# Output projection as seven half-size products of 512 columns, with two weight sums and the adds of x in accumulating DMAs

## The chip, the cores and the metric

The kernel runs on one core of one Trainium2 chip. The metric is the device time of one execution in microseconds (us). Before the change the median of three runs is 432.96 us (432.49 to 433.72). The profile is one more execution, taken by the hardware profiler: its time is 432.8 us, and the span that the profile covers is 431.1 us, so 1.7 us lie around the span.

## What is computed

One decoder block on x of 512 rows and 1024 columns, all float32. The reference, cut to what the change touches:

```python
proj = rms_norm(x, norm_g) @ w_in            # queries, keys, values, gates
y_fox, y_moba = ...                          # two attention branches, 512 x 512 each
merged = (sigmoid(ga + b_gate[0]) * (y_fox @ w_fox)
          + sigmoid(gb + b_gate[1]) * (y_moba @ w_moba))   # 512 x 1024
x = x + merged @ w_out                       # w_out: 1024 x 1024
```

The change is about the last line: the product of `merged` (512 x 1024) with `w_out` (1024 x 1024), and the add of x.

## The kernel before

Every matrix product is done in three matmuls. Each float32 operand is split in a high part and a low part (ScalarE copies to the matmul type `F32R`, VectorE subtracts), and high x high, high x low and low x high are added up in PSUM. A weight piece is 128 partitions x 4 rows of k x 256 columns (512 KB). Its raw form is tagged `wr` (4 buffers), its two parts `wh` and `wl` (4 buffers each). `split` at line 131 makes the parts: line 134 on ScalarE, line 136 on VectorE. `stream` and `pump` keep the list of loads (SP queue) and splits in order and ahead of use.

The kernel has stages: projections, attention with projections in between, "gates" (the groups GA0, GA1, GB0, GB1) and "end". The groups of the gates (`group`, line 703) already compute a product of half-size blocks by seven products in place of eight (Strassen-Winograd): the sums S1 to S4 of the activations lie ready in tiles `S0h` to `S3l`, and the sums of the weights are made in place by VectorE at line 711. Each of their matmuls has 256 columns.

The wm units (`unit_m`, line 807) multiply the second branch by `w_moba` into a PSUM bank `pm` (12 matmuls of 512 columns a unit), VectorE multiplies by the gate and adds the first branch (lines 813 and 814), and ScalarE and VectorE split the result in the parts `mgh` and `mgl` (lines 819 and 820). The eight column blocks of `merged` are so kept in `MG[0]` to `MG[7]`, transposed, 128 x 512 each; blocks 0, 1, 4, 5 come from wm0 and wm2 in stage "gates", and blocks 2, 3, 6, 7 from wm1 and wm3 in stage "end".

The output product follows. `w_out` is taken in four column blocks of 256 (wo0 to wo3), each in two pieces. `first_o` (line 824) does wo0 into four banks at once, block by block as `merged` becomes ready; `unit_o` (line 838) does the rest, one bank of 128 rows x 256 columns after the other. That is 4 column blocks x 4 row blocks x 8 blocks of k x 3 = 384 matmuls of 256 columns, named `po`. `out_o` (line 853) loads a piece of x on the SP queue, adds it to the bank on VectorE (line 857) and stores it from ScalarE's queue (line 858), 128 KB each.

A scheduler orders the instructions of an engine when the program is built; on the chip each engine takes its queue in that order, and an instruction that waits holds all behind it.

Of the kernel before, what the change touches and what calls it, by code (L numbers as in the profile page):

```python
# [19 lines left out]
CW = 256  # L20
# [3 lines left out]
WR = 4  # L24
# [5 lines left out]
def fox_moba_kernel(ctx: ExitStack, tc, xT, x, w_in, w_fl, w_fox, w_moba, w_out, cst, rope, out):  # L30


    nc = tc.nc
    V, A, G, T = nc.vector, nc.scalar, nc.gpsimd, nc.tensor

    con = ctx.enter_context(tc.tile_pool(name="con", bufs=1))
    sb = ctx.enter_context(tc.tile_pool(name="sb", bufs=1))
# [3 lines left out]
    stage = {}  # L41
# [46 lines left out]
    cs = con.tile([P, C_END], F32, name="cs")  # L88
# [17 lines left out]
    for i in range(WARM):  # L106
# [10 lines left out]
    Gh = con.tile([P, KT, S], F32R, name="Gh")  # L117
    Gl = con.tile([P, KT, S], F32R, name="Gl")
# [10 lines left out]
    chunks = {}  # L129

    def split(src, n, name, half=False):
        hi = sb.tile([P, 4, 264], F32R, name=f"wh_{name}", tag="wh", bufs=4)
        lo = sb.tile([P, 4, 264], F32R, name=f"wl_{name}", tag="wl", bufs=4)
        A.activation(hi[:, :, 0:n], src, AF.Copy)  # L134
        for eng, q in ((V, slice(0, 2)), (G, slice(2, 4))) if half else ((V, slice(0, 4)),):
            eng.tensor_tensor(out=lo[:, q, 0:n], in0=src[:, q], in1=hi[:, q, 0:n].bitcast(F32), op=OP.subtract)  # L136
        return hi, lo
# [24 lines left out]
    COLS = {}  # L162
# [13 lines left out]
    loads, preps, first_prep = [], [], {}  # L176
    done = {"loads": 0, "preps": 0}

    def pump(i):

        while True:
            j = done["loads"]
            if j < len(loads) and (j < WR or loads[j - WR][1] < done["preps"]):
                loads[j][0]()
                done["loads"] += 1
            elif done["preps"] < len(preps) and done["preps"] <= i + 3:
                preps[done["preps"]]()
                done["preps"] += 1
            else:
                return  # L190

    def stream(name):
        first_prep[name] = len(preps)
        if name[0] == "G":
            group(name)
            return
        w, n, cnt = ((w_fox, int(name[2]), 1) if name[:2] == "wf" else (w_moba, int(name[2]), 1) if name[:2] == "wm"
                     else (w_out, int(name[2]), 2) if name[:2] == "wo" else (w_in, COLS[name] // CW, 2))
        for hf in range(cnt):
            raw = {}  # L200

            def load(hf=hf, raw=raw):
                raw[0] = sb.tile([P, 4, CW], F32, name=f"wr_{name}{hf}", tag="wr", bufs=WR)
                nc.sync.dma_start(out=raw[0], in_=w[n, :, 4 * hf:4 * hf + 4, :])

            def prep(hf=hf, raw=raw):
                chunks.setdefault(name, []).append(split(raw[0], CW, f"{name}{hf}", HALF[0] and name[1] in "qkvz"))
            loads.append((load, len(preps)))
            preps.append(prep)
# [4 lines left out]
    r = con.tile([P, NT], F32, name="r")  # L214
# [33 lines left out]
    HT = S // 2  # L248
# [420 lines left out]
    FS, MG = {}, {}  # L669

    def br_mm(p, name, br, c):
        hi, lo = chunks[name][0]
        cc = slice(c * P, (c + 1) * P)
        for k in range(4):
            yh, yl = Y[br, k]
            T.matmul(p, hi[:, k, cc], yh, start=(k == 0), stop=False)  # L676
            T.matmul(p, hi[:, k, cc], yl, start=False, stop=False)  # L677
            T.matmul(p, lo[:, k, cc], yh, start=False, stop=(k == 3))  # L678
# [14 lines left out]
    SG = {}  # L693
# [7 lines left out]
    groups = {}  # L701
# [104 lines left out]

    def unit_m(i, c):
        def go():
            j = 2 * i + c
            p = pj(f"pm{j}")  # L810
            br_mm(p, f"wm{i}", "m", c)
            u = SG[i][:, c, :]
            V.tensor_tensor(out=u, in0=p, in1=u, op=OP.mult)
            V.tensor_tensor(out=u, in0=u, in1=FS[i][:, c, :], op=OP.add)
            if i % 2:
                mh_, ml_ = (stage["pool"].tile([P, S], F32R, name=f"mg{hl}{j}", tag="mg", bufs=8) for hl in "hl")
            else:
                mh_, ml_ = (t2("y", 15, f"mg{hl}{j}", dt=F32R) for hl in "hl")
            A.activation(mh_, u, AF.Copy)
            V.tensor_tensor(out=ml_, in0=u, in1=mh_.bitcast(F32), op=OP.subtract)  # L820
            MG[j] = (mh_, ml_)
        return go

    def first_o():
        banks = [pst(tg, 2, f"po0_{i}") for i, tg in enumerate(("pj", "pj", "lg", "lg"))]
        for kk in range(KT):
            hi, lo = chunks["wo0"][kk // 4]
            gh, gl = MG[kk]
            k = kk % 4
            for t in range(NT):  # L830
                st = slice(t * P, (t + 1) * P)
                T.matmul(banks[t][:, :CW], gh[:, st], hi[:, k, :CW], start=(kk == 0), stop=False)
                T.matmul(banks[t][:, :CW], gh[:, st], lo[:, k, :CW], start=False, stop=False)
                T.matmul(banks[t][:, :CW], gl[:, st], hi[:, k, :CW], start=False, stop=(kk == KT - 1))
        for t in range(NT):
            out_o(banks[t], 0, t)

    def unit_o(n, t):
        def go():
            p = pj(f"po{n}{t}")  # L840
            st = slice(t * P, (t + 1) * P)
            for hf in range(2):
                hi, lo = chunks[f"wo{n}"][hf]
                for k in range(4):
                    kk = 4 * hf + k
                    gh, gl = MG[kk]
                    T.matmul(p[:, :CW], gh[:, st], hi[:, k, :CW], start=(kk == 0), stop=False)  # L847
                    T.matmul(p[:, :CW], gh[:, st], lo[:, k, :CW], start=False, stop=False)  # L848
                    T.matmul(p[:, :CW], gl[:, st], hi[:, k, :CW], start=False, stop=(kk == KT - 1))  # L849
            out_o(p, n, t)  # L850
        return go

    def out_o(p, n, t):
        xr = t2("pt", 4, "xr")[:, :CW]
        nc.sync.dma_start(out=xr, in_=x[t * P:(t + 1) * P, n * CW:(n + 1) * CW])
        o = t2("u", 4, "ot")
        V.tensor_tensor(out=o[:, :CW], in0=p[:, :CW], in1=xr, op=OP.add)  # L857
        nc.scalar.dma_start(out=out[t * P:(t + 1) * P, n * CW:(n + 1) * CW], in_=o[:, :CW])


    order = ["fqa", "fka", "fza", "fzb", "fva", "fqb", "fkb", "fvb", "mqa", "mka", "mva", "mza", "mqb", "mkb", "mvb", "mzb", "wf0", "wf1", "wf2", "wf3",
             "GA0", "GA1", "GB0", "wm0", "wm2",
             "GB1", "wm1", "wm3", "wo0", "wo1", "wo2", "wo3"]
    for nm in order[2:]:
        stream(nm)

    def units(name):
        k = name[:2]
        if k[0] == "G":
            return groups[name]  # L870
        if k == "wf":
            return [unit_f(int(name[2]), c) for c in range(2)]
        if k == "wm":
            return [unit_m(int(name[2]), c) for c in range(2)]
        if k == "wo":
            return [unit_o(int(name[2]), t) for t in range(4)]
# [28 lines left out]
    def seq(names):  # L905
        for u in filler(names):
            u()
# [32 lines left out]
    for n in range(4):  # L940
# [9 lines left out]
        if n == 0:  # L950
            for k in range(4):
                store = []

                at = 3 * k + 5
# [21 lines left out]
            gate[0]()  # L976
    seq(["wm0", "wm2", "GB1"])
    enter("end")
    seq(["wm1", "wm3"])
    pump(first_prep["wo0"])  # L980
    first_o()
    seq(["wo1", "wo2", "wo3"])
    stage.pop("guard").__exit__(None, None, None)


# [58 lines left out]
```

## Time and profile before

| | before |
|---|---|
| median of three runs | 432.96 us |
| time of the profiled execution | 432.8 us |
| its span | 431.1 us |
| TensorE busy | 424.4 us |
| VectorE busy | 308.5 us |
| ScalarE busy | 253.9 us |
| GpSimd busy | 87.8 us |
| first matmul of the output product starts | 373.41 us |
| last matmul of the output product starts | 427.15 us |

The lines of the profile stand with the prediction below. PE is TensorE, PEld its weight loads, DVE is VectorE, ACT is ScalarE, POOL is GpSimd, SP is the engine whose queue issues most loads; POOLq, ACTq and SPq are the queues. A row of the timeline gives the start in us, the duration in us, the engine, the line, the operation, and the output tile with its inputs. A row of the groups ends with the count, then the busy time in us and the mean duration of one in ns, then the idle time before them and what ended it.

### The profile page before, as it was taken

How to read it: one execution, taken by the hardware profiler on the slowest of the kernel's cores; microseconds unless marked ns; L12 is line 12 of the kernel's file. 1: busy time of each engine (PE TensorE's matmuls, PEld its weight loads, DVE VectorE, ACT ScalarE, POOL GpSimd, SP SyncE). 2: the span in 40 equal slices, each digit the busy share in tenths (PEclk: the TensorE clock that was granted, in tenths of full speed). 3: DMA queues.
4: the chain of work that ended last, by engine and by line, in shares of the span. 5: the costliest groups of instructions: out<-in, count | busy, mean ns of one | idle time of the engine just before them, and what ended most of it. 6: DMA issues, size and time to landing. Idle time of an engine off the chain costs nothing.

```text
span 431.1 us, 8090 instructions
## 1 busy us (share of the span) xinstructions
PE 424.4 (98%) x3103; PEld 400.7 (93%) x3103; DVE 308.5 (72%) x551; ACT 253.9 (59%) x488; POOL 87.8 (20%) x108
## 2 busy tenths in 40 slices
PE   8999999999999999999999999999999999999996
PEld 6998899999999998999998888899999989999996
DVE  5669976869979867767856896859897796673311
ACT  4986336876867867667765876647645545531100
POOL 1049200227044650045630103020000000000000
PEclk9999999999999999999999999999999999999999
DMA  7981235236565414304304305271415206525231
GB/s 239 398 296 57 80 116 152 74 103 205 166 209 185 130 45 123 122 3 126 117 15 136 109 13 200 99 263 51 141 55 196 98 2 210 189 95 166 85 94 45
DMA packets 25670, 56.13 MB, mean 130 GB/s; under 512 B 3240, under 2 KB 11872, under 8 KB 25632
## 3 DMA queue, kind: packets, MB, share of 16 engines
q1 hardware_dynamic: 14528, 40.08, 27.8%
q10 hardware_dynamic: 9952, 11.34, 8.8%
q0 software_dynamic: 1152, 4.19, 2.7%
q8 instruction: 24, 0.39, 0.4%
q14 instruction: 14, 0.11, 0.1%
HBM read 46.01 MB, written 6.32 MB: 121 GB/s over the span
## 4 chain that ended last, share of the span: by engine, by line
PE 84%; DVE 7%; DMA 5%; ACT 2%; issue 1%; SPq 1%; DVEq 0%; ACTq 0%
PE pb_GB L750 3%; PE pb_GA L750 3%; PE pb_GA L747 3%; PE pb_GB L749 3%; PE pb_GB L747 3%; PE pb_GA L749 3%; PE po L847 3%; PE po L849 3%; PE po L848 3%; PE pv L608 2%; PE pv L607 2%; PE lg L553 2%; PE lg L552 2%; PE pm L676 2%; PE pm L677 2%; PE pm L678 2%
## 5 line engine op out<-in xcount | busy, mean ns | idle before, releaser
L331 POOL TENSOR_TENSOR ff<-ss,mh 128x8 f32<-128x8 f32 x16 | 28.6, 1793 | 65.6 <-DVE ss L329 65.1
L557 ACT ACTIVATE p<-p,negm 128x128 f32<-128x128 f32 (+1 forms) x64 | 35.7, 559 | 9.7 <-DVE negm L555 8.2
L555 DVE CUSTOM_DVE_ANT_0 p<-lg,mask 128x128 f32<-128x128 f32 (+1 forms) x64 | 30.9, 485 | 14.4 <-PE lg L553 13.7
L847 PE MATMUL po<-wh_wo,mgh 128*128 128x256 f32 x96 | 27.1, 282 | 0.0
L849 PE MATMUL po<-wh_wo,mgl 128*128 128x256 f32 x96 | 27.0, 282 | 0.0
L848 PE MATMUL po<-wl_wo,mgh 128*128 128x256 f32 x96 | 27.0, 281 | 0.0
L857 DVE TENSOR_TENSOR ot<-po,xr 128x256 f32<-128x256 f32 x16 | 6.6, 424 | 24.7 <-PE po L849 23.5
L136 DVE TENSOR_TENSOR wl_GA<-wr_ga,wh_GA 128x1024 fp32r<-128x1024 f32 x14 | 17.9, 1294 | 5.7 <-ACT wh_GA L134 3.6
L134 ACT ACTIVATE wh_wo<-wr_wo 128x1024 fp32r<-128x1024 f32 x8 | 8.5, 1061 | 21.6 <-PE po L849 8.0
L552 PE MATMUL lg<-KH,QS 128*128 128x128 f32 (+1 forms) x64 | 20.5, 329 | 0.0
L134 ACT ACTIVATE wh_GA<-wr_ga 128x1024 fp32r<-128x1024 f32 x14 | 14.6, 1059 | 9.2 <-PE pb_GA L749 4.6
L136 DVE TENSOR_TENSOR wl_GB<-wr_gb,wh_GB 128x1024 fp32r<-128x1024 f32 x14 | 16.8, 1222 | 4.2 <-ACT wh_GB L134 3.3
L134 ACT ACTIVATE wh_GB<-wr_gb 128x1024 fp32r<-128x1024 f32 x14 | 14.6, 1060 | 8.6 <-PE pm L677 2.5
L633 DVE TENSOR_TENSOR ypair<-pv,ysh 64x512 f32<-64x512 f32 x16 | 11.0, 688 | 11.2 <-ACT ysh L632 11.0
L847 PEld LDWEIGHTS po<-wh_wo,mgh 128*128 128x128 f32 x96 | 18.1, 189 | 0.0
L848 PEld LDWEIGHTS po<-wl_wo,mgh 128*128 128x128 f32 x96 | 18.1, 189 | 0.0
L849 PEld LDWEIGHTS po<-wh_wo,mgl 128*128 128x128 f32 x96 | 18.1, 188 | 0.0
L136 DVE TENSOR_TENSOR wl_wo<-wr_wo,wh_wo 128x1024 fp32r<-128x1024 f32 x8 | 9.8, 1222 | 7.4 <-ACT wh_wo L134 7.4
L604 DVE TENSOR_TENSOR ptl<-p_a,pth 128x512 fp32r<-128x512 f32 x16 | 11.0, 686 | 4.7 <-ACT pth L603 4.7
L526 DVE SCALAR_TENSOR_TENSOR QS<-p_qT,cs,QS 64x512 fp32r<-64x512 f32 x16 | 12.0, 750 | 2.5 <-ACT QS L525 2.1
L750 PE MATMUL pb_GA<-Gh,wl_GA 128*128 128x256 f32 x48 | 13.6, 283 | 0.0
L749 PE MATMUL pb_GA<-Gl,wh_GA 128*128 128x256 f32 x48 | 13.5, 281 | 0.0
(447 smaller groups left out, 1764.5 us busy)
## 6 DMA issues: line engine op xcount, KB each, us to landing
wr_ga<-in_w_in_dram SPq DMA_DIRECT2D x8, 512.0 KB, 3.5
wr_gb<-in_w_in_dram SPq DMA_DIRECT2D x8, 512.0 KB, 4.1
wr_wo<-in_w_out_dram SPq DMA_DIRECT2D x8, 512.0 KB, 3.8
xt<-in_xT_dram SPq DMA_DIRECT2D x8, 256.0 KB
x<-in_x_dram SPq DMA_DIRECT2D x8, 256.0 KB, 7.5
KH<-KH ACTq DMA_DIRECT2D x16, 128.0 KB, 2.4
s_dramh<-sum_sh ACTq DMA_DIRECT2D x8, 256.0 KB
s_draml<-sum_sl ACTq DMA_DIRECT2D x8, 256.0 KB, 3.5
```

The costliest lines, as they stand in the source:

```text
L134: A.activation(hi[:, :, 0:n], src, AF.Copy)
L136: eng.tensor_tensor(out=lo[:, q, 0:n], in0=src[:, q], in1=hi[:, q, 0:n].bitcast(F32), op=OP.subtract)
L331: G.tensor_tensor(out=f2, in0=ss.rearrange("p t h -> p (t h)"), in1=mh, op=OP.pow)
L552: T.matmul(lg[:, :n], qs[:, qt], kh[:, :n], start=True, stop=False)
L555: V.tensor_tensor_reduce(pt, lg[:, :n], mask[:, 512 - n:512], -0.125, 3.0e38, op0=OP.add, op1=OP.min, accum_out=mkn[:, hh, i:i + 1])
L557: A.activation(pt, pt, AF.Exp, bias=mkn[:, hh, i:i + 1], scale=-1.0, accum_out=rs[:, hh, i:i + 1])
L747: T.matmul(o, hi[:, k, cc], lh, start=(n < 3 and c == 0 and k == 0), stop=False, skip_group_check=True)
L749: T.matmul(o, hi[:, k, cc], ll, start=False, stop=False, skip_group_check=True)
L750: T.matmul(o, lo[:, k, cc], lh, start=False, stop=(k == 3), skip_group_check=True)
L847: T.matmul(p[:, :CW], gh[:, st], hi[:, k, :CW], start=(kk == 0), stop=False)
L848: T.matmul(p[:, :CW], gh[:, st], lo[:, k, :CW], start=False, stop=False)
L849: T.matmul(p[:, :CW], gl[:, st], hi[:, k, :CW], start=False, stop=(kk == KT - 1))
```

## The change

The output product is computed in half-size blocks: `merged` in four blocks A11 to A22 of 256 rows x 512 of k, and `w_out` in four blocks of 512 x 512. Seven products take the place of eight. Four of them have sums of the blocks of `merged` on the left (S1 to S4), four have sums of the blocks of `w_out` on the right (T1 to T4). The left block is the stationary operand, and one matmul takes 512 columns of the right block, which lie as two runs of 256 in the weight tile. There are 7 x 2 x 4 x 3 = 168 of them.

- VectorE makes S1 to S4 from the merged blocks (`sum_o`: 8 subtractions or adds of 128 x 512), ScalarE and VectorE split them (`parts_o`: 8 each) into the tiles `Gh` and `Gl`, which held the normalised input until then.
- `T1` = B12 - B11 and `T3` = B22 - B12: ScalarE negates the raw piece in place, and a DMA issued from GpSimd adds the other block from `w_out` to it in memory (`minus`; 4 DMAs of 512 KB). `T2` = B22 - T1 and `T4` = B21 - T2 are made by VectorE (`sub`; 4 of 128 x 1024).
- The raw pieces are 8 loads of 512 KB as before, four of them into four new buffers of the stage "end" (tag `wx`). There are 14 splits of weight pieces in place of 8.
- ScalarE copies a block's PSUM banks to a tile `eo` (`keep`; 8 of 128 x 512), a DMA from GpSimd adds the piece of x to it (8 of 256 KB), and VectorE adds the last PSUM bank to that (`result`), from where it is stored. The 16 loads of x on the SP queue are gone. The last store is cut in two halves, of which the second goes out from SP.
- Of the merged blocks 0 to 3 only 256 rows are still split; blocks 4 to 7 as before.
- Part of the work is kept behind VectorE's last instruction of the moment (`behind()`), which ties the order in its queue.

```diff
@@ def unit_m: cut in merge_a (matmuls, lines 813 and 814) and merge_b (split)
+            n = HT if j < 4 else S
...
+            A.activation(mh_, u[:, 0:n], AF.Copy)
+            V.tensor_tensor(out=ml_, in0=u[:, 0:n], in1=mh_.bitcast(F32), op=OP.subtract)
...
-    def first_o():
...
-    def unit_o(n, t):
...
-    def out_o(p, n, t):
...
+    def sum_o(m, what):
+        a, b = SG[m], SG[m + 2]
+        x, y, op = {"S1": (a[:, :, HT:S], b[:, :, HT:S], OP.add), "S2": (SF.get((m, "S1")), a[:, :, 0:HT], OP.subtract),
+                    "S4": (b[:, :, 0:HT], SF.get((m, "S2")), OP.subtract),
+                    "S3": (a[:, :, 0:HT], a[:, :, HT:S], OP.subtract)}[what]
...
+        V.tensor_tensor(out=f, in0=x, in1=y, op=op)
+    def parts_o(m, what):
+        f = SF[m, what]
+        hi, lo = (so(what, q)[:, 2 * m:2 * m + 2, :] for q in range(2))
+        A.activation(hi, f, AF.Copy)
+        V.tensor_tensor(out=lo, in0=f, in1=hi.bitcast(F32), op=OP.subtract)
+    O_PRODUCTS = (("A11", "11", 1), ("A12", "21", 2), ("S4", "22", 4), ("S3", "T3", 3), ("S2", "T2", 1),
+                  ("S1", "T1", 1), ("A22", "T4", 3))
...
+        def minus(key, c, plus):
+            A.activation(R[key, c], R[key, c], AF.Copy, scale=-1.0)
+            G.dma_start(out=dst(key, c), in_=src(plus, c), accum_op=OP.add)
+        def sub(key, c, x, y):
+            V.tensor_tensor(out=wide(R[key, c]), in0=wide(R[x, c]), in1=wide(R[y, c]), op=OP.subtract)
+        def prep(n, c):
...
+                A.activation(wide(hi), wide(R[key, c]), AF.Copy)
+                V.tensor_tensor(out=wide(lo), in0=wide(R[key, c]), in1=wide(hi).bitcast(F32), op=OP.subtract)
...
+        def product(n):
...
+            for t in range(2):
+                o = b[at][t].rearrange("p (n c) -> p n c", n=2)
+                for k in range(4):
...
+                    T.matmul(o, gh, hi[:, :, r, :], start=(new and k == 0), stop=False, skip_group_check=True)
+                    T.matmul(o, gh, lo[:, :, r, :], start=False, stop=False, skip_group_check=True)
+                    T.matmul(o, gl, hi[:, :, r, :], start=False, stop=(k == 3), skip_group_check=True)
+        def keep(at, tq, cq):
...
+                A.activation(e[at][:, t, :], b[at][t], AF.Copy)
+                t0 = tq * HT + t * P
+                G.dma_start(out=e[at][:, t, :], in_=x[t0:t0 + P, cq * 512:(cq + 1) * 512], accum_op=OP.add)
+        def result(bb, ee, tq, cq, parts=1):
...
+                    V.tensor_tensor(out=o[:, c:c + n], in0=b[bb][t][:, c:c + n], in1=e[ee][:, t, c:c + n], op=OP.add)
+                    eng = nc.scalar if c == 0 else nc.sync
+                    eng.dma_start(out=out[t0:t0 + P, cq * 512 + c:cq * 512 + c + n], in_=o[:, c:c + n])
...
-    seq(["wm1", "wm3"])
-    pump(first_prep["wo0"])
-    first_o()
-    seq(["wo1", "wo2", "wo3"])
+    groups["WO"]()
+    def behind():
+        return tc.issue_after(last_on(mybir.EngineType.DVE))
...
+        evac(2)
+        with behind():
+            sub("22", "22", "11")
+            parts_o(1, "S2")
+        evac(1)
+        prep(4)
+        product(3)
+        evac(3)
+        with behind():
+            parts_o(1, "S1")
+            prep(5)
+        product(4)
+        evac(4)
+        with behind():
+            sub("21", "21", "22")
+        prep(6)
+        product(5)
+        result(1, 4, 0, 1)
+        result(1, 3, 1, 1)
+        product(6)
+        evac(6)
```

More of the change, by code (lines that the diff above doesn't have):

```diff
@@ L196, in stream @@
             return
+        if name == "WO":
+            group_o()
+            return
         w, n, cnt = ((w_fox, int(name[2]), 1) if name[:2] == "wf" else (w_moba, int(name[2]), 1) if name[:2] == "wm"
-                     else (w_out, int(name[2]), 2) if name[:2] == "wo" else (w_in, COLS[name] // CW, 2))
+                     else (w_in, COLS[name] // CW, 2))
         for hf in range(cnt):
@@ L808, in go, with merge_a @@
         def go():
+            merge_a(i, c)
+            merge_b(i, c)
+        return go
+    def merge_a(i, c):
+        if True:
             j = 2 * i + c
@@ L814, in go @@
             V.tensor_tensor(out=u, in0=u, in1=FS[i][:, c, :], op=OP.add)
-            if i % 2:
-                mh_, ml_ = (stage["pool"].tile([P, S], F32R, name=f"mg{hl}{j}", tag="mg", bufs=8) for hl in "hl")
-            else:
[L818 to L822, printed above, removed]
-    def first_o():
[L825 to L836, printed above, removed]
@@ L838, in unit_o @@
-    def unit_o(n, t):
[L839 to L851, printed above, removed]
@@ L853, in out_o, with merge_b @@
-    def out_o(p, n, t):
[L854 to L858, printed above, removed]
+    def merge_b(i, c):
+        if True:
+            j = 2 * i + c
+            u = SG[i][:, c, :]
+            n = HT if j < 4 else S
+            tiles = [stage["pool"].tile([P, S], F32R, name=f"mg{j}{q}", tag="mg", bufs=6) if i % 2
+                     else t2("y", 15, f"mg{j}{q}", dt=F32R) for q in range(n // HT)]
+            mh_, ml_ = (tiles[0][:, 0:HT], tiles[0][:, HT:S]) if j < 4 else tiles
+            A.activation(mh_, u[:, 0:n], AF.Copy)
+            V.tensor_tensor(out=ml_, in0=u[:, 0:n], in1=mh_.bitcast(F32), op=OP.subtract)
+            MG[j] = (mh_, ml_)
@@ new lines, in fox_moba_kernel, with so @@
+    O_AT = {"S3": (0, HT), "S1": (0, 0), "S2": (4, 0), "S4": (4, HT)}
+    def so(what, hl):
+        k, c = O_AT[what]
+        return (Gh, Gl)[hl][:, k:k + 4, c:c + HT]
+    SF = {}
+    def sum_o(m, what):
[3 more added lines that the diff above has]
+                    "S3": (a[:, :, 0:HT], a[:, :, HT:S], OP.subtract)}[what]
+        f = SF[m, what] = stage["pool"].tile([P, S], F32, name=f"so_{what}{m}", tag="sf", bufs=4).rearrange("p (k t) -> p k t", t=HT)
+        V.tensor_tensor(out=f, in0=x, in1=y, op=op)
@@ L861, in fox_moba_kernel @@
     order = ["fqa", "fka", "fza", "fzb", "fva", "fqb", "fkb", "fvb", "mqa", "mka", "mva", "mza", "mqb", "mkb", "mvb", "mzb", "wf0", "wf1", "wf2", "wf3",
              "GA0", "GA1", "GB0", "wm0", "wm2",
-             "GB1", "wm1", "wm3", "wo0", "wo1", "wo2", "wo3"]
+             "GB1", "wm1", "wm3", "WO"]
     for nm in order[2:]:
@@ L873, in units @@
         if k == "wm":
-            return [unit_m(int(name[2]), c) for c in range(2)]
-        if k == "wo":
-            return [unit_o(int(name[2]), t) for t in range(4)]
+            i = int(name[2])
+            return [unit_m(i, c) if i % 2 == 0 else (lambda c=c: merge_a(i, c)) for c in range(2)]
         if k[1] == "z":
@@ L978, in fox_moba_kernel @@
     enter("end")
-    seq(["wm1", "wm3"])
-    pump(first_prep["wo0"])
-    first_o()
-    seq(["wo1", "wo2", "wo3"])
+    groups["WO"]()
+    prep, product, evac, sub, result = (groups[k] for k in ("prep", "product", "evac", "sub", "out"))
+    def behind():
+        return tc.issue_after(last_on(mybir.EngineType.DVE))
+    m1, m3 = filler(["wm1"]), filler(["wm3"])
+    if True:
+        m1[0]()
+        prep(0)
+        m1[1]()
+        for what in ("S1", "S2", "S4", "S3"):
+            sum_o(0, what)
+        merge_b(1, 0)
+        m3[0]()
+        parts_o(0, "S4")
+        parts_o(0, "S3")
+        merge_b(1, 1)
+        prep(1)
+        prep(2, (0,))
+        m3[1]()
+        parts_o(0, "S2")
+        parts_o(0, "S1")
+        pump(10 ** 6)
+        merge_b(3, 0)
+        product(0)
+        evac(0)
+        merge_b(3, 1)
+        for what in ("S1", "S2", "S4"):
+            sum_o(1, what)
+        with behind():
+            prep(2, (1,))
+        parts_o(1, "S4")
+        product(1)
+        sum_o(1, "S3")
+        parts_o(1, "S3")
+        prep(3)
+        product(2)
+        evac(2)
[11 more added lines that the diff above has]
+        evac(4)
+        with behind():
+            sub("21", "21", "22")
[5 more added lines that the diff above has]
+        evac(6)
     stage.pop("guard").__exit__(None, None, None)
```

74 lines of the change are left out of this document (added).

## The prediction

> **What bounds the kernel now.** I read the page from the top, then the table by stretches of the last 60 us, then the timeline of TensorE there, row by row.
>
> ```profile
> span 431.1 us, 8090 instructions
> PE 424.4 (98%) x3103; PEld 400.7 (93%) x3103; DVE 308.5 (72%) x551; ACT 253.9 (59%) x488; POOL 87.8 (20%) x108
> PEclk9999999999999999999999999999999999999999
> PE 84%; DVE 7%; DMA 5%; ACT 2%; issue 1%; SPq 1%; DVEq 0%; ACTq 0%
> ...
> 370.00:380.00 10.00, 10.00 (x63) 8.89 (x62) 7.05 (x9) 4.17 (x7) 0.00 (x0) 1.00 0.52 167
> 380.00:390.00 10.00, 10.00 (x73) 9.40 (x72) 6.01 (x9) 3.39 (x4) 0.00 (x0) 1.00 0.31 107
> 400.00:410.00 10.00, 10.00 (x86) 10.00 (x86) 3.54 (x5) 2.12 (x2) 0.00 (x0) 1.00 0.33 104
> 420.00:432.00 12.00, 7.43 (x63) 7.23 (x61) 1.27 (x3) 0.00 (x0) 0.00 (x0) 0.89 0.13 44
> ```
>
> TensorE holds 84% of the chain that ended last, at full granted clock. In the changed stretch it is busy for all of every 10 us (second number of a row), while VectorE has 3.5 to 7 us of work (fourth) and ScalarE 0 to 4 (fifth). So a matmul removed there shortens the end, until one of the other queues is late.
>
> ```profile
> 373.41 0.28 PE L832 MATMUL po<-wh_wo,mgh 128*128 128x256 f32 x1
> 381.11 0.40 PE L676 MATMUL pm<-yhm,wh_wm 128*128 128x512 f32 x1
> 383.66 0.39 PE L678 MATMUL pm<-yhm,wl_wm 128*128 128x512 f32 x1
> 383.89 0.28 PE L832 MATMUL po<-wh_wo,mgh 128*128 128x256 f32 x1
> 427.15 0.28 PE L849 MATMUL po<-wh_wo,mgl 128*128 128x256 f32 x1
> 427.47 0.42 DVE L857 TENSOR_TENSOR ot<-po,xr 128x256 f32<-128x256 f32 x1 [2.44 <-PE po L849]
> 427.93 0.34 ACTq L858 DMA_DIRECT2D out_dram<-ot  x1
> ```
>
> The time between starts is what a matmul costs. Twelve of 512 columns fill 381.11 to 383.89: 0.2317 each. From the first output matmul (373.41) to the last (427.15) lie 383 steps of 256 columns and the 36 matmuls of three wm units (36 x 0.2317 = 8.34): (53.74 - 8.34) / 383 = 0.1185 each. Behind the last start come the add on VectorE, the store at 427.93, and 3.17 us to the end of the span.
>
> **The change part by part: TensorE.** Up to 373.41 the queue holds the same matmuls, two products of the gates exchanged; I count nothing. After it 384 of 256 columns leave and 168 of 512 come. The last would start at 373.41 + 8.34 + 167 x 0.2317 = 420.44 in place of 427.15: -6.71. It lasts 0.12 longer (0.40 against 0.28): +0.12. The last add is cut in two halves, and the second store waits for the second half, 0.34 more (its row below, less the 0.08 by which neighbours overlap): +0.34. The final store is 128 KB as now, and I keep the 3.17. Sum -6.25: span 424.9, time 432.8 - 6.25 = 426.6.
>
> One thing in it has no row: the moving operand now lies in two runs of 256 columns. Below 0.2317 no row of 512 columns goes, which excludes a gain; above, two matmuls of 256 cost 0.237, so at most 168 x 0.0053 = 0.9 us more. I take 0.2317, since the operation has that width, and keep 0.9 for the range.
>
> **VectorE's queue.**
>
> ```profile
> 345.63 0.68 DVE L813 TENSOR_TENSOR uGB<-pm,uGB 128x512 f32<-128x512 f32 x1
> 346.24 1.23 DVE L136 TENSOR_TENSOR wl_GB<-wr_gb,wh_GB 128x1024 fp32r<-128x1024 f32 x1
> 347.38 1.22 DVE L711 TENSOR_TENSOR wr_gb<-wr_gb,wr_gb 128x1024 f32<-128x1024 f32 x1
> ...
> L857 DVE TENSOR_TENSOR ot<-po,xr 128x256 f32<-128x256 f32 x16 | 6.6, 424 | 24.7 <-PE po L849 23.5 <-PE po L834 1.2
> L814 DVE TENSOR_TENSOR uGB<-uGB,f 128x512 f32<-128x512 f32 x8 | 5.5, 689 | 0.1
> L820 DVE TENSOR_TENSOR mgl<-uGB,mgh 128x512 fp32r<-128x512 f32 x8 | 5.5, 687 | 0.2
> ```
>
> Starts show 0.61 for 512 elements and 1.14 for 1024. Behind 373.41 the changed queue has 13 weight splits and 4 weight subtractions (17 x 1.14 = 19.4), 6 left sums, 8 left splits, 6 gate operations, 2 merge splits and 7 adds of results (29 x 0.61 = 17.7), and 4 of 256 (1.4): 38.5 us of work in 47. On average it fits. The tight place is the run behind the last wm unit. Counting 0.2317 a matmul from 373.41 in the new order, that unit ends as number 55, near 386.5. From there VectorE has, without a pause, 7 operations of 512 (4.3, and 0.4 for pairs that wait for each other), one split (1.1), one left sum (0.6), the two splits of T3 and the two subtractions that make T2 (4.6), and two left splits (1.2): 12.2 us, done at 398.8. TensorE wants the last of these as number 118, at 400.75. Slack 2.0 us, and the next uses have more. I cost VectorE at nothing; what hides it is TensorE's own work, and if VectorE were 16% slower in this run, the cover would be gone.
>
> **ScalarE, POOL and the accumulating DMAs.** This is the step with a new wait.
>
> ```profile
> 353.32 0.61 ACT L819 ACTIVATE mgh<-uGB 128x512 fp32r<-128x512 f32 x1
> 353.89 1.06 ACT L134 ACTIVATE wh_GB<-wr_gb 128x1024 fp32r<-128x1024 f32 x1
> 357.51 1.07 ACT L757 ACTIVATE e_GB<-pb_GB 128x512 f32<-128x512 f32 x2
> 368.30 1.06 ACT L134 ACTIVATE wh_wo<-wr_wo 128x1024 fp32r<-128x1024 f32 x1 [1.04 <-PE pb_GB L749]
> 369.27 0.89 ACT L793 ACTIVATE uGB<-uGB,cs 128x256 f32<-128x256 f32 x2
> 373.53 1.06 ACT L134 ACTIVATE wh_wo<-wr_wo 128x1024 fp32r<-128x1024 f32 x1 [3.37 <-issue]
> ...
> L279 POOL DMA_DIRECT2D S0l<-s_draml x1 | 0.5, 543 | 0.0
> S1h<-s_dramh POOLq DMA_DIRECT2D x1, 512.0 KB, 3.5
> S1l<-s_draml POOLq DMA_DIRECT2D x1, 512.0 KB, 4.3
> S2h<-s_dramh POOLq DMA_DIRECT2D x1, 512.0 KB, 5.8
> S3h<-s_dramh POOLq DMA_DIRECT2D x1, 512.0 KB, 6.3
> wr_wo<-in_w_out_dram SPq DMA_DIRECT2D x8, 512.0 KB, 3.8
> ...
> 359.13 11.85 SPq L204 DMA_DIRECT2D wr_wo<-in_w_out_dram  x5
> ```
>
> Starts show 0.57 for 512 and 0.97 for 1024. The split that starts at 373.53 is where ScalarE stands at the same point of the new order (a split of the second weight piece, released by the same matmul). Behind it come six more of 1024 (weight splits and the negations, 7 x 0.97 = 6.8 with itself), four left parts (2.3) and three short ones (1.1): both pieces of T3 are negated by 382.7 and 383.7. Their raw loads stand on SP among those that now go out from 359.13 to 371, into buffers of their own; with 3.8 for a landing and some 1.5 more for each of three that are in flight before, they are there by 379. POOL issues each add in 0.54.
>
> T3's split on ScalarE waits for the first add. Behind it in ScalarE's order stand two left parts, the two copies of the first product's banks, the split of the second piece and one left part (together 4.8 us), and TensorE wants that last part as number 98, at 396.1. So the first add must have landed by 391.3, or 8.6 us behind the negation. The first add of x (behind the bank copies, done near 392.9) holds VectorE's add of a result, and behind that stands the split of T2, wanted as number 134 at 404.5; less 2.4 us of VectorE's work that leaves 9.1. T1's adds have over 20 us, and the other adds of x about 8 or more.
>
> No row shows an adding DMA. From below it lands like a copy from POOL, 3.5; from above like twice the slowest copy, 12.6. I take the range from 5 to 8: the copies issued one behind the other land at 3.5, 4.3 and 5.8, so another 512 KB of reading adds 1 to 2 us. That is under 8.6, and the wait is hidden: nothing. At 12.6 it isn't: 4.0 too late at T3, then 3.5 at the first add of x, which ScalarE's order has already put back, then some 4 at the adds before the last results: +11.5.
>
> [...]
>
> **What moves for nothing.** The 16 loads of x leave SP's queue; the eight raw loads stay. ScalarE's queue issues eight stores in place of 16, and the rest of its added work (six splits, the negations, 8 left parts, 8 copies) lies in the idle that the rows by stretches show. The merge splits of blocks 0 to 3 shrink to 256 columns: a gain for VectorE alone, hidden.
>
> **The rivals.**
>
> A. Slower: the adding DMAs are slow and become the bound, at ScalarE's split of T3, VectorE's add of the first result and the last adds. It decides from the landing at which three delays of L - 8.8 pay back 6.25: L = 10.9. At 12.6 the sum is -6.25 + 11.5: 438. For it: no row excludes it, 8 more of them carry x, and all stand in one POOL queue. Against it: the slowest copy took 6.3.
>
> B. The adds are late, but less, be it by their landing or by a late issue in POOL's queue: L from 8.6 to 10.9. Then the gain is partly given back, 427 to 433; at 9.8, three times 1.0: 429.6.
>
> [...]
>
> D. The change doesn't do what it says on TensorE, since two runs of columns are paid as two matmuls: 0.9 us less, 427.5. It is within the forecast.
>
> **How the numbers follow.** The forecast, all waits hidden, has 0.60, with its own range 425.8 to 427.7. A has 0.19, B 0.12, C 0.09. The profiled execution (432.8) stands 0.16 below the median, so I say 426.7. The range must take in most of B and C to leave out no more than 2 in 10: 425.6 to 432.0. What cannot be told from no change is 0.3%, 1.3 us: the forecast, most of C and over half of B are faster (0.60 + 0.09 + 0.07 = 0.76), the rest of B is the same (0.05), and A is slower (0.19).
>
> **What would show it.** Right: TensorE busy for the whole of every stretch behind 373, matmuls of the output at 0.232 from start to start, the last one starting near 420.4; the wait for ScalarE's T3 split without a DMA as its releaser. A or B: ScalarE idle before that split, or VectorE before an add of a result, with a DMA named, landings over 8.6, and gaps on TensorE near 396 or 404. [...] The forecast is wrong if the matmuls of two runs start more than 0.237 apart, or if the time behind the last matmul grows by more than 1 us.

## The result, and the profile after

The changed kernel takes 427.01 us, the median of four runs (426.54 to 427.16), beside 433.32 us for the kernel before in the same group (432.49 to 433.72). The ratio is 0.9855, with a 95% interval of 0.9837 to 0.9873: faster by about 1.5%, well over the 0.3% that can be told. The forecast was 426.7 us.

| | before | forecast | after |
|---|---|---|---|
| time of the profiled execution, us | 432.8 | 426.6 | 427.16 |
| its span, us | 431.1 | 424.9 | 425.3 |
| first matmul of the output starts, us | 373.41 | 373.41 | 373.77 |
| last matmul of the output starts, us | 427.15 | 420.44 | 420.99 |
| from the first to the last, us | 53.74 | 47.03 | 47.22 |

The first rows of the page after, the chain of waits among them, and the table by stretches (columns: length, then busy us and count for TensorE, weight loads, VectorE, ScalarE, GpSimd; granted clock; DMA share; GB/s):

```profile
span 425.3 us, 7669 instructions
PE 418.5 (98%) x2887; PEld 387.7 (91%) x2887; DVE 327.2 (77%) x570; ACT 271.4 (64%) x514; POOL 98.4 (23%) x120
...
PE 96%; DVE 2%; DMA 1%; issue 0%; ACT 0%; SPq 0%; DVEq 0%; ACTq 0%
```

```profile
373.40:380.00 6.60, 6.60 (x32) 5.44 (x31) 5.52 (x9) 6.15 (x10) 1.46 (x2) 1.00 1.01 281
380.00:390.00 10.00, 10.00 (x45) 8.09 (x44) 9.28 (x14) 6.93 (x10) 2.44 (x2) 1.00 0.84 148
390.00:400.00 10.00, 10.00 (x45) 8.06 (x44) 9.96 (x13) 5.63 (x9) 1.79 (x2) 1.00 0.44 72
400.00:410.00 10.00, 10.00 (x44) 8.06 (x43) 8.21 (x9) 6.04 (x9) 3.48 (x5) 1.00 0.65 133
```

TensorE now holds 96% of the chain and is busy for the whole of every stretch, at full granted clock. VectorE has filled up: 9.28 and 9.96 of 10 us from 380 to 400, where it had 6.0 in the first of the two before. So the time is again the number of matmuls by what each costs, but the cover above them has become thin. Rows of the timeline after, of all engines:

```profile
372.38 1.28 POOL L888 DMA_DIRECT2D wr_o<-in_w_out_dram  x1 [87.26 <-ACT wr_o L887]
373.77 0.40 PE L938 MATMUL po<-wh_o,mg 128*128 128x512 f32 x1
...
381.71 2.00 ACT L887 ACTIVATE wr_o<-wr_o 128x1024 f32<-128x1024 f32 x2
383.06 2.44 POOL L888 DMA_DIRECT2D wr_o<-in_w_out_dram  x2 [3.62 <-ACT wr_o L887]
386.95 0.69 DVE L822 TENSOR_TENSOR uGB<-pm,uGB 128x512 f32<-128x512 f32 x1 [0.69 <-PE pm L681]
389.30 1.06 ACT L901 ACTIVATE wh_o<-wr_o 128x1024 fp32r<-128x1024 f32 x1 [0.22 <-PE po L940]
392.78 1.06 ACT L901 ACTIVATE wh_o<-wr_o 128x1024 fp32r<-128x1024 f32 x1
395.48 2.35 DVE L891 TENSOR_TENSOR wr_o<-wr_o,wr_o 128x1024 f32<-128x1024 f32 x2
397.75 1.89 DVE L860 TENSOR_TENSOR Gl<-so_S,Gh 128x512 fp32r<-128x512 f32 x3
...
404.91 0.40 PE L939 MATMUL po<-wl_o,Gh 128*128 128x512 f32 x1
412.40 0.39 PE L939 MATMUL po<-wl_o,Gh 128*128 128x512 f32 x1
416.12 0.39 PE L939 MATMUL po<-wl_o,mg 128*128 128x512 f32 x1
420.99 0.39 PE L940 MATMUL po<-wh_o,mg 128*128 128x512 f32 x1
421.41 0.76 DVE L956 TENSOR_TENSOR ot<-po,eo 128x256 f32<-128x256 f32 x2 [1.39 <-PE po L940]
422.20 0.36 SPq L958 DMA_DIRECT2D out_dram<-ot  x1
```

Line 901 is the weight split on ScalarE, 887 the negation, 888 the adding DMA of a weight piece, 891 the subtraction of weights on VectorE, 860 a left part, 956 the add of a result. The split of T3 at 389.30 waited 0.22 us, for a matmul and not for a DMA, and its second piece at 392.78 for nothing. The adding DMAs by the issues, and the landings of the four that carry weights:

```profile
wr_o<-in_w_out_dram POOLq DMA_DIRECT2D x4, 512.0 KB, 7.5
eo<-in_x_dram POOLq DMA_DIRECT2D x8, 256.0 KB, 5.0
```

```profile
DMA to landing us min/median/max: 5.8/7.5/10.2
```

### The profile page after: what moved, and what is told of

The parts are those of the page before. It is cut to its first block, busy times and chain, and to the rows that moved or that the text cites. A ratio compares the mean times of both kernels' runs of the same rounds, so it can differ in the third digit from the quotient of the medians.

```text
span 425.3 us, 7669 instructions
## 1 busy us (share of the span) xinstructions
PE 418.5 (98%) x2887; PEld 387.7 (91%) x2887; DVE 327.2 (77%) x570; ACT 271.4 (64%) x514; POOL 98.4 (23%) x120
## 4 chain that ended last, share of the span: by engine, by line
PE 96%; DVE 2%; DMA 1%; issue 0%; ACT 0%; SPq 0%; DVEq 0%; ACTq 0%
PE pb_GB L753 3%; PE pb_GA L753 3%; PE pb_GB L750 3%; PE pb_GA L750 3%; PE pb_GB L752 3%; PE pb_GA L752 3%; PE po L939 3%; PE po L938 3%; PE po L940 3%; PE pv L611 2%; PE pv L610 2%; PE lg L556 2%; PE lg L555 2%; PE pm L681 2%; PE pm L680 2%; PE pm L679 2%
## 5 line engine op out<-in xcount | busy, mean ns | idle before, releaser
L334 POOL TENSOR_TENSOR ff<-ss,mh 128x8 f32<-128x8 f32 x16 | 26.7, 1678 | 65.2 <-DVE ss L332 64.7
L888 POOL DMA_DIRECT2D wr_o<-in_w_out_dram x4 | 4.9, 1293 | 95.5 <-ACT wr_o L887 95.5
L901 ACT ACTIVATE wh_o<-wr_o 128x1024 fp32r<-128x1024 f32 x14 | 14.8, 1059 | 10.0 <-PE pb_GB L752 2.8
L902 DVE TENSOR_TENSOR wl_o<-wr_o,wh_o 128x1024 fp32r<-128x1024 f32 x14 | 16.9, 1221 | 3.8 <-ACT wh_o L901 3.8
L136 DVE TENSOR_TENSOR wl_GB<-wr_gb,wh_GB 128x1024 fp32r<-128x1024 f32 x14 | 16.9, 1222 | 3.5 <-ACT wh_GB L134 3.5
L635 ACT ACTIVATE ysh<-pv 64x512 f32<-64x512 f32 x16 | 9.5, 593 | 6.7 <-PE pv L611 5.6
L750 PE MATMUL pb_GA<-Gh,wh_GA 128*128 128x256 f32 x48 | 13.5, 281 | 0.0
L753 PE MATMUL pb_GB<-Gh,wl_GB 128*128 128x256 f32 x48 | 13.5, 281 | 0.0
L752 PE MATMUL pb_GB<-Gl,wh_GB 128*128 128x256 f32 x48 | 13.4, 281 | 0.0
L679 PE MATMUL pf<-yhf,wh_wf 128*128 128x512 f32 x32 | 13.1, 408 | 0.4 <-DVE zs_mzb L425 0.4
L528 ACT ACTIVATE QS<-p_qT,cs 64x512 fp32r<-64x512 f32 x16 | 10.9, 681 | 3.8 <-PE lg L555 2.0
```

Source lines behind the costliest of these rows:

```text
L334: G.tensor_tensor(out=f2, in0=ss.rearrange("p t h -> p (t h)"), in1=mh, op=OP.pow)
L750: T.matmul(o, hi[:, k, cc], lh, start=(n < 3 and c == 0 and k == 0), stop=False, skip_group_check=True)
L752: T.matmul(o, hi[:, k, cc], ll, start=False, stop=False, skip_group_check=True)
L753: T.matmul(o, lo[:, k, cc], lh, start=False, stop=(k == 3), skip_group_check=True)
L901: A.activation(wide(hi), wide(R[key, c]), AF.Copy)
L902: V.tensor_tensor(out=wide(lo), in0=wide(R[key, c]), in1=wide(hi).bitcast(F32), op=OP.subtract)
```

## The experiments

All are edits of the changed kernel. In the table, "stretch" is the time from the first to the last start of an output matmul in the profile, and "gaps" is what the timeline shows of TensorE standing idle in it. A median without a ratio is a single run.

| run | median, us | ratio to before, 95% interval | stretch, us | gaps, us |
|---|---|---|---|---|
| the changed kernel | 427.01 | 0.9855 (0.9837 to 0.9873) | 47.22 | none |
| T3's block added twice | 433.99 | | 53.59 | 3.30 |
| first x added twice | 426.70 | | 47.22 | none |
| three more VectorE operations | 426.73 | | 47.36 | none |
| six more | 433.55 | | 53.55 | 4.48 |
| T1 and T3 by VectorE | 428.59 | 0.9902 (0.9880 to 0.9923) | 48.88 | 0.93 |
| x added by VectorE | 433.45 | 1.0008 (0.9998 to 1.0019) | 53.24 | 3.98 |
| no adding DMA | 435.95 | 1.0077 (1.0051 to 1.0104) | 56.35 | 6.42 |
| VectorE's order untied | 432.67 | 0.9993 (0.9971 to 1.0015) | 51.58 | 2.13 |
| the changed kernel again | 426.84 | 0.9862 (0.9848 to 0.9877) | 47.22 | none |
| x by VectorE, reordered | 427.85 | 0.9883 (0.9863 to 0.9903) | 47.53 | none |
| two matmuls of 256 | 427.65 | 0.9880 (0.9863 to 0.9896) | 47.98 | none |
| last bank in two | 427.01 | 0.9863 (0.9846 to 0.9881) | 47.35 | none |

**How much cover the adding DMAs have.** The wait that rivals A and B were built on is made longer.

```diff
             for c in range(2):
                 minus("12", c, "22")
+            for c in range(2):
+                G.dma_start(out=dst("12", c), in_=src("22", c), accum_op=OP.add)
```

> The block B22 is added to each piece of T3 twice, one add behind the other (T3 is then 2 B22 - B12), so that the wait of ScalarE's T3 split is some 6 to 7 us longer and all else is as in the changed kernel. Forecast by the prediction's slack (the first add must have landed by 391.3): the first piece's first add was issued at 383.1 in the changed kernel and landed 5.8 to 8.2 later; the second lands another 6 to 7 later, near 396.5. That is 5 us too late: 427.0 + 5 = 432 (431 to 433), with a DMA as the releaser of ScalarE before the T3 split and a gap on TensorE near 396. Rival, that the cover is much larger than worked out: under 1 us, 427 to 428, and no gap.

Measured: 433.99 us. The timeline of this run and its table by stretches:

```profile
383.30 1.06 ACT L887 ACTIVATE wr_o<-wr_o 128x1024 f32<-128x1024 f32 x1 [0.26 <-DMA wr_o<-in_w_out_dram]
...
395.13 1.06 ACT L901 ACTIVATE wh_o<-wr_o 128x1024 fp32r<-128x1024 f32 x1 [4.56 <-DMA wr_o<-in_w_out_dram]
398.64 1.06 ACT L901 ACTIVATE wh_o<-wr_o 128x1024 fp32r<-128x1024 f32 x1 [0.97 <-DMA wr_o<-in_w_out_dram]
...
400.27 0.79 PE L940 MATMUL po<-wh_o,Gh 128*128 128x512 f32 x1 [3.30 <-ACT Gh L859]
...
404.28 0.63 PE L941 MATMUL po<-wl_o,Gh 128*128 128x512 f32 x1
404.70 0.63 PE L942 MATMUL po<-wh_o,Gl 128*128 128x512 f32 x1
```

```profile
402.00:404.00 2.00, 2.00 (x6) 1.52 (x6) 2.00 (x4) 1.06 (x1) 0.00 (x0) 0.50 0.25 43
404.00:406.00 2.00, 2.00 (x7) 1.52 (x6) 2.00 (x4) 0.00 (x0) 0.00 (x0) 0.50 0.02 4
407.00:408.00 1.00, 1.00 (x6) 0.81 (x5) 0.58 (x2) 0.75 (x1) 0.00 (x0) 1.00 0.39 150
```

The place and the deadline hold. The output stretch starts 0.64 us later here than in the profile of before (374.05 against 373.41), so the limit of 391.3 becomes 391.9; the first piece was split at 395.13, 3.2 late (forecast: 5), and TensorE stood still for 3.30, before a matmul that waits for the left part behind T3's second split in ScalarE's order (that split waited another 0.97 for its own piece). But the stretch grew by 53.59 - 47.22 = 6.4 us, so that a shorter delay than forecast still came out over the forecast range of 431 to 433 us. Nearly all of the other 3.1 is TensorE's clock: behind the gap it was granted 0.50, and matmuls started 0.43 us apart (404.28 to 404.70) in place of 0.23, until about 406.4. So this late wait cost its length and then about as much again.

```diff
             for t in range(2):
                 A.activation(e[at][:, t, :], b[at][t], AF.Copy)
                 t0 = tq * HT + t * P
                 G.dma_start(out=e[at][:, t, :], in_=x[t0:t0 + P, cq * 512:(cq + 1) * 512], accum_op=OP.add)
+            for t in range(2) if at == 1 else ():
+                t0 = tq * HT + t * P
+                G.dma_start(out=e[at][:, t, :], in_=x[t0:t0 + P, cq * 512:(cq + 1) * 512], accum_op=OP.add)
```

> The first piece of x is added twice (two DMAs of 256 KB more; that block of the output then holds 2x). Forecast by the prediction's slack of 9.1 us behind the bank copies (done at 392.9, so landed by 402.0): the first pair is issued from 392.7 on and lands 3.7 to 7.4 us later, the second pair as long behind that, 402 to 406: 0 to 4 us late, 427 to 431, most likely 429, with a DMA before VectorE's add of the first result. Rival, that what stands behind that add is wanted later than worked out: 427.0, VectorE idle before the add but no gap on TensorE.

Measured: 426.70 us, the stretch unchanged. VectorE's rows of the timeline show the wait:

```profile
399.87 0.69 DVE L959 TENSOR_TENSOR ot<-po,eo 128x512 f32<-128x512 f32 x1 [0.86 <-DMA eo<-in_x_dram]
...
402.24 0.69 DVE L959 TENSOR_TENSOR ot<-po,eo 128x512 f32<-128x512 f32 x1 [0.54 <-DMA eo<-in_x_dram]
```

The second adds landed 3.7 to 3.9 us behind their issue, faster than I had taken them, so VectorE was held until 399.9 and 402.2, just at the worked-out limit of 402.0, and nothing was lost. That agrees with a slack of about 9 us but doesn't exceed it: where the loss begins stays open. (The scheduler also put a split of T2 between the two adds here, at 400.48, which in the changed kernel stands behind both, so the queue is not quite the same.)

**How much cover VectorE has.** One left sum is repeated at the head of its tight run, three times and six times:

```diff
-        V.tensor_tensor(out=f, in0=x, in1=y, op=op)
+        for _ in range(4 if (m, what) == (1, "S1") else 1):
+            V.tensor_tensor(out=f, in0=x, in1=y, op=op)
```

> VectorE makes one left sum of the second half of k (S1) four times in place of once, at the head of its tight run: three more operations of 512 elements, 3 x 0.61 = 1.8 us. The prediction gave that run 2.0 us of slack: nothing is lost, 427.0 (426.5 to 427.5). Rival, that VectorE is already the bound there: all 1.8 us, 428.8.

> The same left sum seven times, six more operations, 6 x 0.61 = 3.7 us in VectorE's tight run. By the slack of 2.0 us: 3.7 - 2.0 = 1.7 lost, 428.7, with a gap on TensorE before the matmuls of S4 or T3. Rival 1, that the slack is larger: 427.0. Rival 2, that the run behind it (T2's sums and splits) has none left either and the delay is passed on in full or more: 430.7 or over.

Three more cost 0.14 us of the stretch. But that does not show that 1.8 us fit into the slack of 2.0, since the scheduler answered the longer queue with another order. VectorE's rows in the run with three more:

```profile
396.94 1.22 DVE L892 TENSOR_TENSOR wr_o<-wr_o,wr_o 128x1024 f32<-128x1024 f32 x1
398.07 1.28 DVE L861 TENSOR_TENSOR Gl<-so_S,Gh 128x512 fp32r<-128x512 f32 x2
...
399.88 1.21 DVE L892 TENSOR_TENSOR wr_o<-wr_o,wr_o 128x1024 f32<-128x1024 f32 x1
```

One of the two subtractions that make T2 now stands behind two of the left parts, and these start 25.02 us behind the start of the stretch, against 23.98 in the changed kernel: 1.0 us later, and TensorE did not wait for them. The rest of the slack wasn't tried. With six the stretch grew by 6.3 us, not by 1.7, and the order changed further: the adds of the first result came to stand ahead of the left sums S2 and S4, and waited there for their pieces of x. Two rows of its timeline:

```profile
396.38 0.69 DVE L957 TENSOR_TENSOR ot<-po,eo 128x512 f32<-128x512 f32 x1 [2.11 <-DMA eo<-in_x_dram]
...
400.68 1.11 PE L939 MATMUL po<-wh_o,Gh 128*128 128x512 f32 x2 [4.23 <-ACT Gh L860]
```

VectorE stood for 2.1 us in the very run that was made to be too full, so its order, and not its room alone, made this loss.

**What the adding DMAs are worth.** First T1 and T3, then x, then both without them:

```diff
-                if n == 0:
-                    minus("11", c, "12")
...
-            for c in range(2):
-                minus("12", c, "22")
...
         m1[1]()
+        sub("11", "12", "11")
+        sub("12", "22", "12")
```

```diff
-                A.activation(e[at][:, t, :], b[at][t], AF.Copy)
                 t0 = tq * HT + t * P
-                G.dma_start(out=e[at][:, t, :], in_=x[t0:t0 + P, cq * 512:(cq + 1) * 512], accum_op=OP.add)
+                nc.sync.dma_start(out=e[at][:, t, :], in_=x[t0:t0 + P, cq * 512:(cq + 1) * 512])
+                V.tensor_tensor(out=e[at][:, t, :], in0=b[at][t], in1=e[at][:, t, :], op=OP.add)
```

> T1 and T3 are made by VectorE, as subtractions of 128 x 1024 in SBUF, in place of the negations on ScalarE and the four adding DMAs: 4 x 1.14 = 4.6 us more on VectorE, 4 x 0.97 less on ScalarE. In the changed kernel VectorE is idle for 1.1 us from 373.4 to 380 and 0.7 to 390, so up to 1.8 are swallowed and 2.8 push the tight run, which has 2.0 of slack (three more operations, 1.8 us, cost nothing). Forecast: 0.8 lost, 427.8 (427 to 429). Rival 1, that VectorE has room enough: 427.0. Rival 2, that a gap of 3 us or more comes on TensorE, which then runs at half its clock behind it as with the T3 block added twice: 431 or more.

> Each piece of x is loaded by SP into the tile eo ahead of time and VectorE adds the bank to it (8 more operations of 512, 8 x 0.61 = 4.9 us), in place of ScalarE's bank copy and the adding DMA. Two of them fall in the tight run near 392 (1.2 of the 2.0 of slack), four near 402 to 405, where VectorE is idle for 1.8 of the 10 us, two near 410. Forecast: 427.5 (427 to 428.5). Rival 1, nothing at all: 427.0. Rival 2, that the run from 400 to 410 has no slack left and what is late there comes through, with half the clock behind a gap of 3 us: 430 or more.

> Both edits together, so seven products with no adding DMA at all: 4.6 + 4.9 = 9.5 us more on VectorE, 38.5 + 9.5 = 48 us of work in the 47 behind 373.4. VectorE is then the bound: the gain of the seven products is mostly given back, 430 to 434 (before: 432.9), with several gaps on TensorE released by VectorE. Rival, that the adding DMAs only moved work that was hidden anyway: 427 to 428.

With T1 and T3 on VectorE 1.6 us are lost, twice the forecast. Only some 0.7 of the 4.6 us more fell into idle time (VectorE was busy for 5.83 of the 7 us to 380 and never idle from there to 390). The other 3.9 less the slack of 2.0 would make 1.9, but that this sum is the cause is not shown: the order changed here too, and the gaps on TensorE, 0.57 and 0.36, waited for parts that ScalarE makes (lines 834 and 859). The stretch grew by 1.66 us for 0.93 of gaps, at a granted clock of 1.00 throughout: a gap is counted from the end of a matmul's record of 0.40 us, but the next matmul was due 0.23 behind its start. With x on VectorE the whole gain is gone, and that forecast was wrong. The timeline of that run:

```profile
402.67 0.69 DVE L948 TENSOR_TENSOR eo<-po,eo 128x512 f32<-128x512 f32 x1 [2.66 <-PE po L940]
403.61 0.69 DVE L948 TENSOR_TENSOR eo<-po,eo 128x512 f32<-128x512 f32 x1 [0.24 <-PE po L940]
404.21 2.35 DVE L891 TENSOR_TENSOR wr_o<-wr_o,wr_o 128x1024 f32<-128x1024 f32 x2
...
410.15 0.67 PE L939 MATMUL po<-wl_o,Gh 128*128 128x512 f32 x1 [2.79 <-DVE wl_o L902]
```

VectorE stood for 2.66 us before an add that waits for the banks of the S4 product, with the two subtractions of T2 behind it: they start at 404.21, against 395.48 in the changed kernel. I had counted work against idle time; what decided was which instruction stood behind a waiting one. Without any adding DMA the losses add up: 435.95 us, slower than before the change and over the forecast of 430 to 434. Its order was left as it came, so what all the adding DMAs together are worth in a good order stays open.

**The order by itself.**

```diff
     def behind():
-        return tc.issue_after(last_on(mybir.EngineType.DVE))
+        return ExitStack()
```

> The four ties of VectorE's order are taken out, with the same instructions. The run with six more operations showed what an order by the scheduler can do: a result's add stood ahead of the left sums, waited 2.1 us for its piece of x, and TensorE stood still for 4.2 us. Forecast: something of the sort here too, 429 to 432, with a gap on TensorE between 396 and 406. Rival, that with 2.0 us of slack the order does not matter: 427.0.

Measured: 432.67 us, just over the forecast of 429 to 432, and a ratio of 0.9993: with the same instructions, untied, nothing of the gain is left. Its ten runs lie far apart, from 429.94 to 434.73. The timeline and one stretch of this run:

```profile
399.51 0.73 PE L938 MATMUL po<-wh_o,Gh 128*128 128x512 f32 x2 [0.75 <-ACT wh_o L901]
401.34 0.50 PE L939 MATMUL po<-wl_o,Gh 128*128 128x512 f32 x1 [1.10 <-DVE wl_o L902]
...
426.92 1.35 DVE L956 TENSOR_TENSOR ot<-po,eo 128x512 f32<-128x512 f32 x3 [2.80 <-DMA out_dram<-ot]
```

```profile
403.00:404.00 1.00, 1.00 (x4) 0.81 (x3) 1.00 (x2) 0.16 (x1) 0.00 (x0) 0.50 0.00 0
```

Three parts make the loss. The gaps are 2.13 us. The stretch grew by another 51.58 - 47.22 - 2.13 = 2.2 us, of which about 1.5 go with the clock: it stood at 0.50 behind the second gap, and eight matmuls there started 0.43 us apart. And the results come so late in VectorE's order that the last adds wait 2.80 us for a store to free its buffer: from the last matmul (425.16) to the end (431.8) pass 6.6 us in place of 4.3.

If order and not room was what x on VectorE lacked, then exchanging two lines, with x on VectorE as above, must bring the time back:

```diff
-        evac(2)
         with behind():
             sub("22", "22", "11")
             parts_o(1, "S2")
+        evac(2)
```

> As with x added by VectorE, the same instructions, but the two subtractions that make T2 and the left parts behind them are put ahead of the adds of x that wait for the S4 product's banks. In the run with x added by VectorE, VectorE stood for 2.7 us before such an add, from 400.0 to 402.7, with T2 queued behind it. If that order took the gain, the time comes back to 427 to 428, with no gap on TensorE over 0.5 us. Rival, that VectorE is too full with 4.9 us more: about 433, as before.

Measured: 427.85 us, against 433.45 without the exchange and 426.84 for the changed kernel in the same group. In its table VectorE is busy for all of the 10 us from 400 to 410, and TensorE too:

```profile
400.00:410.00 10.00, 10.00 (x45) 8.01 (x44) 10.00 (x14) 3.30 (x4) 0.00 (x0) 1.00 0.14 53
```

In the profiles the adding DMAs for x buy 0.3 us of the stretch (47.53 against 47.22). The other 1.6 of the longer span lie ahead of it: the stretch begins at 374.84 against 373.25, and TensorE was behind early on, with 281 matmuls in the first 50 us against 288. What the adding DMAs for x do is take an add that waits for TensorE out of VectorE's queue, and the order of the program can do that too.

**The terms of the sum.** The changed kernel was run once more beside these:

> The changed kernel as it is, beside the others of this group: 427.0 (426.5 to 427.3).

```diff
-                    T.matmul(o, gh, hi[:, :, r, :], start=(new and k == 0), stop=False, skip_group_check=True)
...
+                    for n2 in range(2):
+                        T.matmul(o[:, n2], gh, hi[:, n2, r, :], start=(new and k == 0), stop=False, skip_group_check=True)
...
```

> Each of the 168 matmuls of 512 columns is cut in two of 256, one for each run of columns: 336 x 0.1185 = 39.8 us in place of 168 x 0.2326 = 39.1 (203 steps took 47.22 us in the changed kernel): 0.7 more, 427.8. Rival D, that two runs are paid as two matmuls anyway: 0 to 0.3 more.

Measured: 427.65 us against 426.84, and a stretch of 47.98, 0.76 more. (The sums that this kernel returns are not those of the block, from a cause that is not known; the work on TensorE is as described, each matmul of 512 columns in two of 256.) Rival D is out: two runs of columns in one matmul are not paid as two. It also splits the gain: 427.65 against 433.01 is what seven products in place of eight bring, with all that comes with them, 5.4 us, and some 0.8 are the wider matmuls.

```diff
+            if new and at == 3:
+                b[at] = [pst("pj", 2, "po30"), (pst("pj", 2, "po31"), pst("tp", 3, "po32"))]
...
+                if (at, t) == (3, 1):
+                    for q in range(2):
+                        for k in range(4):
...
+                            o = b[at][t][q][:, :CW]
+                            T.matmul(o, gh, hi[:, q, r, :], start=(new and k == 0), stop=False, skip_group_check=True)
...
```

> The second row block of the last result gets two PSUM banks, one for each 256 columns, and its matmuls of 256 columns run half by half (48 of 256 in place of 24 of 512: 5.69 - 5.56 = 0.13 more), so that the first half is added while the second is multiplied. The last matmul is 0.12 shorter, and only one add of 256 stands behind it in place of two (0.34 less): 0.13 - 0.12 - 0.34 = -0.33, 426.7 against 427.0 for the changed kernel of this group. Rival, that the end hangs on the store and nothing moves: 427.0 to 427.2.

Measured: 427.01 us against 426.84: no difference that can be told. The timeline shows that the step itself was right:

```profile
420.98 0.28 PE L944 MATMUL po<-wh_o,mg 128*128 128x256 f32 x1
421.30 0.42 DVE L973 TENSOR_TENSOR ot<-po,eo 128x256 f32<-128x256 f32 x1 [0.88 <-PE po L944]
421.75 0.36 SPq L975 DMA_DIRECT2D out_dram<-ot  x1
```

The stretch is 0.13 longer, and from the last start to the end (424.8) pass 3.82 us, against 4.33 in the changed kernel of the same group (420.47 to 424.8): 0.38 less in all. But the stretch began at 373.63 here and at 373.25 there, and this difference ahead of the changed part ate it. No version was found that is faster than the changed kernel by more than can be measured.

## Why the prediction was right, and where it was not

- **TensorE, the sum.** Right. 203 steps took 47.22 us, forecast 47.03, and the end behind the last start 4.31, forecast 4.4. The 0.19 too little is the term for a matmul of 512 columns: where the stationary operand comes from `Gh` and `Gl` it is (412.40 - 404.91) / 32 = 0.2341, with the `mg` tiles (420.99 - 416.12) / 21 = 0.2319, the row of before. Why, no run tried. The two runs of columns cost nothing; 0.9 was kept for them.
- **The start.** I counted nothing ahead of 373.41; it was 373.77. In the thirteen profiles of the changed kernel and its variants, which have nearly the same work up to there, that start lies between 373.05 and 374.84, and in the two of the changed kernel itself at 373.77 and 373.25. So most of it seems to be how executions differ, and a gain of a few tenths drowns in it.
- **VectorE.** The working came out closely: the second of the three left parts from 397.75 on, two steps of 0.61 later, ends at 399.0 (forecast 398.8), and nothing waited for it. That the slack is 2.0 is not shown: each run that was to take it up came out in another order. With three more operations these left parts came 1.0 later at no loss, and more was not tried cleanly.
- **ScalarE and the adding DMAs.** The negations end at 383.7 as forecast, T3's split did not wait for a DMA, and that split was where a longer landing cost time (3.2 us late, a gap of 3.30). Two margins were thin. The raw loads were to be there by 379, but with T3's block added twice one of them held the second negation until 383.30. And T3's second piece, for which the prediction has no limit, landed 8.2 us behind its issue at 384.0, 0.6 before its split at 392.78. The durations were off: an issue took 1.19 to 1.49 us (median 1.24) where I took 0.54 from a copy of the same size, and the landings were 5.8 to 10.2 us where I took 5 to 8. The 10.2 fell on the piece of T1 issued at 372.38, beside a DMA share of 1.01 from 373.4 to 380; T1 had over 20.
- **The rivals' prices.** Here a step failed: A and B priced a late wait at its own length ("three times 1.0"). T3's block added twice shows 3.30 us of gap and 6.4 lost. The losses behind B's 429.6 could have been up to twice as large, and the point from which A decides would then lie lower than the landing of 10.9. The chances also hold 0.09 for C, in which slower operations make VectorE the bound. No run shows such a term: the 14 weight splits of 128 x 1024 on VectorE mean 1217 to 1223 ns in the thirteen profiles of the changed kernel and its variants, against 1222 for the eight in the profile of before.
- **What the prediction left out.** It worked out the run of VectorE in the order as built, and so came out right, but gave that order no price. Untied it is 432.67: the tie carries as much of the result as the eighth product that left (5.7 us against 5.4). A chance that the order would not hold, with its price, should have been among the rivals.

## What to carry to other kernels

When TensorE is the bound, count its matmuls for the gain, and then walk the queue of the fullest helper engine instruction by instruction: a sum of busy time says little, and what stands behind an instruction that waits for TensorE or a DMA says nearly all. An accumulating DMA, or a mere exchange of two lines, can take such an instruction out of the way (here 426.84 and 427.85 us against 433.45), and an order that is left to the scheduler (untied, 432.67) should be read again after every edit. Price a gap on TensorE at more than its length: in these runs it cost 1.4 to 2 times that (6.3 us of stretch for 4.48 of gaps, 6.4 for 3.30, and 1.7 for 0.93 without a lowered clock).

## What the hardware showed that was not expected

- **The clock behind a gap.** A gap of 3.30 us (T3's block added twice) was followed by 6 us at a granted clock of 0.50, and one of 4.23 (six more VectorE operations) by 3.4; two gaps of 0.75 and 1.10 within 2.6 us (order untied) were followed by some 3.4 us of it; 0.57 and 0.36 close together (T1 and T3 by VectorE) by none, and 0.96, 0.46 and 1.00 spread over some 6 us (the run without adding DMAs) by none. So 1.85 us in two short gaps lowered the clock, and 2.42 us in three did not: the idle time alone does not tell. What sets it off, and for how long, no run here shows. In the ten runs of the untied kernel the mean granted clock goes from 0.990 in the slowest (434.73 us) to 1.000 in the fastest (429.94).
- **The issue of an adding DMA.** 1.19 to 1.49 us of GpSimd for 512 KB, against 0.54 for seven of the eight copies in the profile of before (0.77 for the first). Whether the adding or the shape of the copy makes it wasn't tried.
